# First forms of head 0 and 1 traced ahead of z's, plain output weights loaded as the quads' are, gates loaded behind the last value product: one core, a bidirectional encoder block

## The chip, the cores and the metric

The kernel runs on one core of one Trainium2 chip. The metric is the device time of a launch in microseconds (us). TensorE is called PE, VectorE DVE, ScalarE ACT, GpSimd POOL and SyncE SP; PEld are PE's weight loads.

## The reference

One layer of an encoder on 512 tokens of width 1024, in float32:

```python
h = rmsnorm(x, g_mix);  proj = h @ w_in          # xc, gb, gc, q, k, v, g_sw, gate_a, gate_r
y_a = (gb * dwconv3(gc * xc)) @ w_a_out
ret = retention_fwd(q, k, v) + retention_bwd(q, k, v)       # 4 heads: 256 wide q, k; 512 wide v
ret = (ret - mean) * rsqrt(var + EPS) * g_ret               # per head
y_r = (ret * silu(g_sw)) @ w_r_out                          # 2048 x 1024
x = x + (sigmoid(gate_a) * y_a + sigmoid(gate_r) * y_r) @ w_o
x = x + (silu(h2 @ w_ff_gate) * (h2 @ w_ff_up)) @ w_ff_down # h2 = rmsnorm(x, g_ffn)
return rmsnorm(x, g_final)
```

The change concerns the way to y_r: the value products of the heads, and their output product with w_r_out.

## The kernel before

Every float32 operand is split in two rounded halves, hi and lo (`split`: ACT casts the hi, L217, DVE subtracts for the lo, L218; with a column of scales L220 and L221). A product is three matmuls: hi hi, hi lo, lo hi. Large products run as Strassen's forms, each a sum or difference of blocks that is split in its turn. A matmul of 128x128 by 128x512 is the common one.

**Weights.** `plan` (L64) lists all weight units in the order of use. A quad's unit ("q") comes from the packed array `wquad`: `load_raws` issues its loads on SP's queue ahead of use, up to LEAD (4) entries and more past the one that is being split, into a pool of ten raw tiles (512 KB each). A plain block ("c") comes from `wpack`: `prefetch_block` issues its two loads (L262) at the moment at which it is its turn to be split, two units (AHEAD) before use. Split units (whi, wlo) have five buffers each.

**Queues.** SP's queue carries the loads, and the 16 transfers that turn a head's result into columns (`transpose`, L241, "big<-turned"). POOL's queue carries the stores of z (L668), the accumulating loads of weight sums (L294 to L296), the loads of z's forms (L1054) and the gates A. The framework gives SP's transfers eight semaphores in turn, and a transfer waits until the one before it on its semaphore has landed; it also orders the instructions of each engine, near to the order in which they are traced, and `tc.issue_after` holds an instruction behind another. What is traced first on ACT and DVE is mostly done first, and each engine runs its list in order.

**The stage of the change**, by PE's products in order, with the matmuls of each: scores of head 3 (`do_scores`), `mix_b(3)` (L1094, the last of the convolution's projections, whose results go through `z_forms`), a11 (L1097, 24), a12 (L1100, 24), the value product of head 3 (`do_pv`, L1105, 48), the plain product of head 2 with the right half of its weights (`token_major`, L1110, 48), s1, s2, s3, s4 (24 each), head 2 with the left half (L1131, 48), a22 (24), head 3 with the right half (L1144, 48) and with the left half (L1148, 48); then the products of z (y_a). a11, a12, s1 to s4 and a22 are Strassen's forms of heads 0 and 1 with w_r_out's first 1,024 rows; heads 2 and 3 use its other rows plainly.

- `first_forms` (L1010) makes a11 and a12: two casts on ACT, two subtractions on DVE (128x1024 each). `sum_forms` (L1017) makes s1 and s2, `last_forms` (L1030) s3, s4 and a22.
- `do_pv` normalises each of its four banks: statistics (L967 to L969), the power on POOL (L970), L976 on DVE, which reads the bank for the last time, and L978 on ACT. A bank is free for the next product after L976. `do_t` turns the result on DVE (L238) and on SP (L241), `split_t` splits it with the group norm's gain (L220, L221).
- `leave` (L1117) copies s2's and later s3's banks on ACT (L1119) and subtracts on DVE (L1121).
- `sgr` are the swish gates of the branch R, 8 transfers of 256 KB on SP (`load_turned`, L934, "big<-gr"), traced behind the first `leave`.

Of the kernel before, what the change touches and what calls it, by code (L numbers as in the profile page):

```python
# [17 lines left out]
P = 128  # L18
# [4 lines left out]
HEADS = 4  # L23
QK = 256
VD = 512
# [23 lines left out]
LEAD = 4  # L49
# [2 lines left out]

WIDTH = {"w": 512, "x": 256, "a": 512, "o": 512, "f": 256, "g": 512, "r": 512, "d": 512}
FORMS = ("b11", "t1", "t2", "b21", "t3", "t4", "b22")

EARLY_FORMS = ("b11", "b21", "t1", "t2", "t3", "t4", "b22")
# [5 lines left out]
def plan():  # L64

    out = []

    def a(name, col):
        out.append(("c", name, 0, 8, col, 256))

    def b(name, row, nk, col, nc):
        out.append(("c", name, row, nk, col, nc))

    def quad(c0, c1):
        for name in FORMS:  # L80
            for u in (0, 2):
                out.append(("q", ("w", c0, c1), name, u, 2))

    for h in range(EARLY):
        for r in (0, 512):
            b("w_in", r, 4, (C_Q + h * QK, C_K + h * QK), 512)
    for h in range(HEADS):
        quad(C_V + h * VD, C_G + h * VD)
        if h >= EARLY:
            a("w_in", C_Q + h * QK)  # L90
            a("w_in", C_K + h * QK)
    for c in (0, 512):
        quad(C_GA + c, C_GR + c)
    for c0, c1 in ((C_XC, C_GC), (C_XC + 256, C_GC + 256), (C_GB, C_GB + 256)):
        for name in FORMS:
            out.append(("q", ("x", c0, c1), name, 0, 4))
    for s in (2, 3):
        for c in (C_XC, C_GC, C_GB):
            a("w_in", c + s * 256)
    def r(*names):  # L100
        for name in names:
            for u in (0, 2):
                out.append(("q", ("r",), name, u, 2))

    r("b11", "b21")
    b("w_r_out", 2 * VD, 4, 512, 512)
    r("t1", "t2", "t3", "b22")
    b("w_r_out", 2 * VD, 4, 0, 512)
    r("t4")
    for c in (512, 0):  # L110
        b("w_r_out", 3 * VD, 4, c, 512)
    for kind, name in [("a", x) for x in FORMS[:6]] + [("o", "b11"), ("a", "b22")] + [
            ("o", x) for x in ("t1", "t2", "b21", "b22", "t3", "t4")]:
        for u in (0, 2):
            out.append(("q", (kind,), name, u, 2))
    def f(q, *names):
        for n in names:
            if q == LONE:
                out.append(("q", ("f", q), n, 0, 4))
            else:  # L120
                for u in (0, 2):
                    out.append(("q", ("g", q), n, u, 2))

    def d(q0, n):
        names = FORMS if q0 + n == NQ else EARLY_FORMS
        units = [(name, u) for name in names for u in range(0, n, 2)]
        if q0 + n == NQ:

            i = units.index(("b21", 2))
            units[i:i + 3] = units[i + 1:i + 3] + units[i:i + 1]  # L130
        for name, u in units:
            out.append(("q", ("d", q0), name, u, min(2, n - u)))

    f(0, "b11", "b21")
    f(1, "b11")
    f(0, "t2", "t1", "t3", "t4", "b22")
    f(1, "t1", "t2", "b21", "t3", "t4", "b22")
    f(2, *FORMS)
    d(*FF_PARTS[0])
    f(3, *FORMS)  # L140
    f(4, *FORMS)
    d(*FF_PARTS[1])
    f(LONE, *FORMS)
    d(*FF_PARTS[2])
    return out
# [39 lines left out]
def block_kernel(ctx: ExitStack, tc: tile.TileContext, xw0, xw, xT, xtok, wpack, wquad, cols, decs, gret_rows, rot, g_ffn, g_final, out):  # L185
    nc = tc.nc
# [14 lines left out]
    def bigtile(dt=F32, n=4):  # L201
        return big.tile([P, n, 512], dt, tag="big", name="big", padded_shape=[P, 4, 512])
# [40 lines left out]
    pos = [0]  # L243
# [148 lines left out]

    def token_major(lhs, pss, start, stop):

        c = Chunk()
        for kk in range(4):
            wh, wl = c.w(kk, 0, 512)
            for nb in range(NB):
                xh, xl = (x[:, nb, kk * P:(kk + 1) * P] for x in lhs)
                for i, (l, r) in enumerate(((xh, wh), (xh, wl), (xl, wh))):  # L400
                    nc.tensor.matmul(pss[nb], l, r, start=start[nb] and kk == 0 and i == 0,  # L401
                                     stop=stop[nb] and kk == 3 and i == 2, skip_group_check=True)
# [58 lines left out]
    def snap(ps):  # L461
        t = t512()
        nc.scalar.copy(t, ps)  # L463
        return t
# [189 lines left out]
    sgd = [kept(f"sg{h}") for h in range(HEADS)]  # L654
    gad = [kept(f"ga{j}") for j in range(2)]
    grd = [kept(f"gr{j}") for j in range(2)]
# [16 lines left out]
    for h in range(EARLY):  # L673
        pss = [bank() for _ in range(4)]
        for kk in range(8):
            if kk % 4 == 0:
                c = Chunk()
# [193 lines left out]
    def mix_b(s, c, mid=None):  # L871
        def ev_b(m, ps):
            nc.vector.tensor_tensor(out=c[:, m], in0=ps, in1=c[:, m], op=ALU.mult)
            if mid and not m:
                mid()
        feature_major(xg, ev_b)
        z_forms(s, c)
# [31 lines left out]
    def load(src, dt=F32):  # L909
        t = bigtile(dt)  # L910
        nc.sync.dma_start(t if dt == F32 else t.bitcast(F32), src)
        return t
# [18 lines left out]
    def load_turned(queue, t, d):  # L931

        for j in range(NB):
            queue.dma_start(t[32 * j:32 * j + 32], d[:, j, :].rearrange("(m r) e -> r m e", m=4))  # L934

    def do_scores(qk, tab):
        p = (bigtile(F32R), bigtile(F32R))
        for mb in range(NB):
            ps = bank()
            for d in range(2):  # L940
                sl = slice(mb * P, (mb + 1) * P)
                mm3(ps, (qk[0][:, 2 + d, sl], qk[1][:, 2 + d, sl]), (qk[0][:, d, :], qk[1][:, d, :]),
                    d == 0, d == 1)
            t = t512()
            o = (3 - mb) * P
            nc.vector.scalar_tensor_tensor(out=t, in0=ps, scalar=QK ** -0.5, in1=tab[:, o:o + 512],
                                           op0=ALU.mult, op1=ALU.mult)
            split(t, p[0][:, mb, :], p[1][:, mb, :])
        return p
# [30 lines left out]
    def do_t(h, t):  # L980
        yr = (bigtile(F32R), bigtile(F32R))
        transpose(lambda b: yr[1].bitcast(F32)[:, b, :], t, True)
        return yr
# [58 lines left out]
    def split_t(h, yr):  # L1042
        with tc.issue_after(hi_of[0].ins), tc.issue_after(low_of[0].ins):
            for eb in range(4):
                hi, lo = (x[:, :, P * eb:P * eb + P] for x in yr)
                split(lo.bitcast(F32), hi, lo, gret[:, 4 * h + eb:4 * h + eb + 1])
# [15 lines left out]
    v, sg, g = load_v(0)  # L1062
    p = do_scores(*qk)
# [3 lines left out]
    c = mix_c(2, us)  # L1067

    qk = load_qk(1)
    v, sg1, g = load_v(1)  # L1070
    do_pv(p, vv, sg)
    p = do_scores(*qk)
# [7 lines left out]
    v, sg2, _ = load_v(2)  # L1080
    do_pv(p, vv, sg1)
    p = do_scores(*qk)
# [3 lines left out]
    c = mix_c(3, us)  # L1086

    do_pv(p, vv, sg2)
    v = load(vd[3], F32R)
    p = do_scores(*qk)  # L1090
    yr2 = do_t(2, sg2)
    sg3 = load(sgd[3])
    vv = split_v(v)
    mix_b(3, c, first_forms)  # L1094

    a, b = ([bank(), bank()] for _ in range(2))
    prod_tm(4, rf["a11"], a, True)  # L1097
    p1 = [snap(x) for x in a]
    split_t(2, yr2)
    prod_tm(4, rf["a12"], b, True, True)  # L1100
    ysum.append(bigtile())
# [1 line left out]
        nc.vector.tensor_tensor(out=ysum[0][:, tt, :], in0=b[tt], in1=p1[tt], op=ALU.add)  # L1103
    sum_forms()
    do_pv(p, vv, sg3)  # L1105
    yr3 = do_t(3, sg3)

    new, old = [True] * NB, [False] * NB
    c, e = ([bank(), bank()] for _ in range(2))
    token_major(yr2, e + c, new, old)  # L1110
    last_forms()
    d = [bank(), bank()]
# [8 lines left out]
            nc.vector.tensor_tensor(out=ysum[1][:, o + tt, :], in0=d[tt], in1=u, op=ALU.subtract)  # L1121
        return copies[-1]
    leave(0)
    sgr = [bigtile(), bigtile()]
    for x, src in zip(sgr[::-1], grd[::-1]):
        load_turned(nc.sync, x, src)
    prod_tm(4, rf["s3"], a, False)
    last = leave(2)
    prod_tm(4, rf["s4"], e, False)
# [1 line left out]
    b = [bank(), bank()]  # L1131
# [121 lines left out]
    a, d, b = po["a"], [bank(), bank()], [bank(), bank()]  # L1253
# [254 lines left out]
    n = FF_PARTS[-1][1]  # L1508
# [111 lines left out]
def pack_quads(w_in, w_a, w_r, w_o, gate, up, down):  # L1620

    out = np.zeros((len(QUARTERS), P, QH), np.float32)
    for i, (_, (kind, *q), name, u, n) in enumerate(QUARTERS):
        r, c = int(name[1]) - 1, int(name[2]) - 1
        if kind in "wx":
            w = w_in.reshape(2, 4, P, -1)[r, u:u + n // WIDTH[kind], :, q[c]:q[c] + WIDTH[kind]]
        elif kind == "a":

            w = w_a.reshape(4, 2, P, 2, 512)[u:u + n // 512, r, :, c]
        elif kind == "r":  # L1630
            w = w_r[0:2 * VD].reshape(2, 4, P, 2, 512)[r, u:u + n // 512, :, c]
        elif kind == "o":
            w = w_o.reshape(2, 4, P, 2, 512)[r, u:u + n // 512, :, c]
        elif kind == "f":
            w = (gate, up)[c].reshape(2, 4, P, NQ, 256)[r, :, :, q[0]]
        elif kind == "g":
            w = (gate, up)[c].reshape(2, 4, P, -1)[r, u:u + n // 512, :, q[0] * 512:q[0] * 512 + 512]
        else:
            w = down.reshape(NQ, 2, P, 2, 512)[q[0] + u:q[0] + u + n // 512, r, :, c]
        out[i, :, :n] = w.transpose(1, 0, 2).reshape(P, n)  # L1640
    return out
# [46 lines left out]
```

## Time and profile before

| what | value |
|---|---|
| time, median of 3 runs | 1032.43 us (1031.98 to 1032.61) |
| the profiled execution's own time | 1030.13 us |
| its span, first to last instruction | 1028.3 us |
| mean granted clock of PE | 0.987 |
| instructions | 13417 |
| bytes moved | 222.70 MB, mean 217 GB/s |
| matmul busy | 1001.4 us, x4722 |

The page cuts the span into 40 slices of 25.7 us; slice 20 of them (from 0 to 39) begins at 514 and slice 23 at 591. A row of the timeline gives the start, the duration, the engine, the line, the operation, output<-input by the program's names, how many instructions it joins (x4), and in brackets the idle time before the first of them and what ended it. Starts of neighbouring rows lie closer than durations, since an instruction starts before the end of the one before. The row of a transfer on SPq or POOLq shows when it was issued; when it landed is told by the issues' view (KB of one, median us to landing) or by what waited for it.

### The profile page before, as it was taken

Reading aid. Unit: us, or ns where it says so; the run is one execution under the profiler, and the core shown is the slowest. Engines: PE = TensorE matmul, PEld = TensorE weight load, DVE = VectorE, ACT = ScalarE, POOL = GpSimd, SP = SyncE. Lnnn points to the kernel's source line nnn. Section 1 sums busy time; section 2 is a strip of 40 time slices with the busy share of each in tenths; the row PEclk is TensorE's granted clock in tenths of the full one; section 3 lists DMA queues with packets and bytes.
Section 4 is the critical chain, followed back from the end, with each engine's and each line's share of the span. In section 5 each row is a group of like instructions: output and inputs, shape, how many; then the busy total and the mean of one; then the engine's idle time right before and its main releaser. Section 6 shows DMA issues by size and latency. Waiting matters only on the chain.

```text
span 1028.3 us, 13417 instructions
## 1 busy us (share of the span) xinstructions
PE 1001.4 (97%) x4722; PEld 836.4 (81%) x4722; DVE 876.5 (85%) x1141; ACT 554.3 (54%) x745; POOL 161.0 (16%) x256
## 2 busy tenths in 40 slices
PE   9999999999999999999699989999999999999996
PEld 7888888888889998888578868888888888888885
DVE  7877998979798988967887349999989996999897
ACT  7547656554665445333545215668655555574655
POOL 0030231222112003131302100011001001003202
PEclk9999999999999999999889989999999999999998
DMA  9525587694867657989748987557776459496953
GB/s 352 196 77 196 172 295 220 206 312 144 274 198 234 246 201 248 402 273 243 223 139 214 328 297 224 166 184 210 200 207 155 171 188 258 116 256 113 267 153 103
DMA packets 65795, 222.70 MB, mean 217 GB/s; under 512 B 10240, under 2 KB 10368, under 8 KB 61632
## 3 DMA queue, kind: packets, MB, share of 16 engines
q1 hardware_dynamic: 46816, 149.46, 42.9%
q0 software_dynamic: 18624, 72.10, 26.7%
q8 instruction: 37, 0.61, 0.2%
q10 hardware_dynamic: 288, 0.29, 0.1%
q14 instruction: 30, 0.25, 0.1%
HBM read 173.83 MB, written 57.41 MB: 225 GB/s over the span
## 4 chain that ended last, share of the span: by engine, by line
PE 82%; DMA 8%; DVE 6%; SPq 1%; issue 1%; ACT 1%; POOL 0%; POOLq 0%; ACTq 0%; DVEq 0%
PE bank L456 56%; PE bank L412 8%; PE bank L376 5%; PE bank L377 5%; PE bank L378 5%; DMA big<-turned 2%; DMA big<-gr 2%; DMA raw<-wpack 2%; DMA big<-ql 2%; SPq L241 1%; DVE wlo L218 1%; DVE raw L323 1%; DVE turned L238 0%; DVE big L1142 0%; DVE big L218 0%
## 5 line engine op out<-in xcount | busy, mean ns | idle before, releaser
L218 DVE TENSOR_TENSOR wlo<-raw,whi 128x1024 fp32r<-128x1024 f32 (+2 forms) x306 | 357.8, 1190 | 98.7 <-ACT whi L217 95.6
L217 ACT CAST whi<-raw 128x1024 fp32r<-128x1024 f32 (+2 forms) x305 | 307.8, 1028 | 235.8 <-PE bank L456 82.1
L456 PE MATMUL bank<-whi,xform 128*128 128x512 f32 x1056 | 330.5, 390 | 0.0
L456 PE MATMUL bank<-whi,big 128*128 128x512 f32 x708 | 224.5, 393 | 10.8 <-ACT big L217 9.7
L456 PEld LDWEIGHTS bank<-whi,xform 128*128 128x128 f32 x1056 | 198.0, 188 | 42.2 <-DVE xform L218 1.0
L456 PE MATMUL bank<-wlo,xform 128*128 128x512 f32 x528 | 205.7, 390 | 0.0
L456 PEld LDWEIGHTS bank<-whi,big 128*128 128x128 f32 x708 | 133.8, 189 | 39.9 <-ACT big L217 10.2
L456 PE MATMUL bank<-wlo,big 128*128 128x512 f32 x354 | 138.9, 392 | 0.1
L323 DVE TENSOR_TENSOR raw<-raw 128x1024 f32<-128x1024 f32 x116 | 136.8, 1198 | 0.7
L456 PEld LDWEIGHTS bank<-wlo,xform 128*128 128x128 f32 x528 | 99.1, 188 | 21.1 <-DVE wlo L218 0.7
L463 ACT COPY t<-bank 128x512 f32<-128x512 f32 x97 | 56.6, 586 | 73.9 <-PE bank L456 59.5
L376 PE MATMUL bank<-big,whi 128*128 128x512 f32 x220 | 85.7, 390 | 0.0
L378 PE MATMUL bank<-big,wlo 128*128 128x512 f32 x220 | 85.6, 389 | 0.0
L377 PE MATMUL bank<-big,whi 128*128 128x512 f32 x220 | 85.6, 389 | 0.0
L456 PEld LDWEIGHTS bank<-wlo,big 128*128 128x128 f32 x354 | 67.2, 190 | 14.5 <-DVE wlo L218 0.6
L412 PE MATMUL bank<-xform,whi 128*128 128x256 f32 x304 | 55.3, 283 | 0.2 <-ACT t L463 0.2
L337 POOL DMA_DIRECT2D raw<-wquad x20 | 17.7, 886 | 210.5 <-ACT t L463 66.4
L378 PEld LDWEIGHTS bank<-big,wlo 128*128 128x128 f32 x220 | 41.3, 188 | 8.6
L376 PEld LDWEIGHTS bank<-big,whi 128*128 128x128 f32 x220 | 41.3, 188 | 8.6
L377 PEld LDWEIGHTS bank<-big,whi 128*128 128x128 f32 x220 | 41.3, 188 | 8.6
L412 PEld LDWEIGHTS bank<-xform,whi 128*128 128x128 f32 x304 | 47.5, 192 | 0.7 <-ACT t L463 0.6
L401 PE MATMUL bank<-whi,big 128*128 128x512 f32 x128 | 41.8, 404 | 4.5 <-ACT whi L217 4.5
(218 smaller groups left out, 1299.1 us busy)
## 6 DMA issues: line engine op xcount, KB each, us to landing
raw<-wquad SPq DMA_DIRECT2D x148, 512.0 KB, 5.3
raw<-wpack SPq DMA_DIRECT2D x34, 512.0 KB, 5.8
raw<-wquad POOLq DMA_DIRECT2D x20, 512.0 KB, 6.7
big<-turned SPq DMA_DIRECT2D x112, 64.0 KB, 4.9
t_g<-wquad POOLq DMA_DIRECT2D x12, 512.0 KB, 8.3
z<-t POOLq DMA_DIRECT2D x24, 256.0 KB, 4.6
t_o<-wquad POOLq DMA_DIRECT2D x12, 512.0 KB, 8.1
zform<-z POOLq DMA_DIRECT2D x6, 1024.0 KB, 13.7
```

The costliest lines, as they stand in the source:

```text
L217: first = (round or nc.scalar.copy)(hi, src)
L218: low_of[0] = nc.vector.tensor_tensor(out=lo, in0=src, in1=hi.bitcast(F32), op=ALU.subtract)
L241: nc.sync.dma_start(out(b)[32 * q:32 * q + 32], ts[q // n][32 * b:32 * b + 32, q % n * 512:(q % n + 1) * 512])
L323: nc.vector.tensor_tensor(out=t, in0=t, in1=raws[quad, more, u][:, 0:n], op=ALU.add)
L337: nc.gpsimd.dma_start(out=t[:, 0:n], in_=src[:, 0:n], accum_op=ALU.add)
L376: nc.tensor.matmul(ps, lh, rh, start=first, stop=False)
L377: nc.tensor.matmul(ps, lh, rl, start=False, stop=False)
L378: nc.tensor.matmul(ps, ll, rh, start=False, stop=last)
L401: nc.tensor.matmul(pss[nb], l, r, start=start[nb] and kk == 0 and i == 0, stop=stop[nb] and kk == 3 and i == 2, skip_group_check=True)
L412: nc.tensor.matmul(o, l[:, c], r[:, k], start=start and s == 0 and k == 0 and i == 0, stop=stop and k == 3 and i == 2, skip_group_check=True)
L456: nc.tensor.matmul(pss[tt], l, r[:, c], start=start and k == 0 and i == 0, stop=stop and k == n - 1 and i == 2, skip_group_check=True)
L463: nc.scalar.copy(t, ps)
```

## The change

Three edits. `first_forms` is called right behind the scores of head 3, no more from within `mix_b(3)`; the load of head 3's gates (sg3) is traced later, behind the copies of a11. The plain blocks of w_r_out become units of a new kind "p" of the quads' array, so that `load_raws` issues their loads ahead. And the gates R (`sgr`) are loaded right behind head 3's value product, ahead of its turning, and `load_raws` is called there once more.

```diff
--- before.py
+++ after.py
@@ -52,7 +52,7 @@
 
 
 
-WIDTH = {"w": 512, "x": 256, "a": 512, "o": 512, "f": 256, "g": 512, "r": 512, "d": 512}
+WIDTH = {"w": 512, "x": 256, "a": 512, "o": 512, "f": 256, "g": 512, "r": 512, "p": 512, "d": 512}
 FORMS = ("b11", "t1", "t2", "b21", "t3", "t4", "b22")
 
 EARLY_FORMS = ("b11", "b21", "t1", "t2", "t3", "t4", "b22")
@@ -103,12 +103,11 @@
                 out.append(("q", ("r",), name, u, 2))
 
     r("b11", "b21")
-    b("w_r_out", 2 * VD, 4, 512, 512)
+    out.extend(("q", ("p", 2, 1), "b11", u, 2) for u in (0, 2))
     r("t1", "t2", "t3", "b22")
-    b("w_r_out", 2 * VD, 4, 0, 512)
+    out.extend(("q", ("p", 2, 0), "b11", u, 2) for u in (0, 2))
     r("t4")
-    for c in (512, 0):
-        b("w_r_out", 3 * VD, 4, c, 512)
+    out.extend(("q", ("p", 3, c), "b11", u, 2) for c in (1, 0) for u in (0, 2))
     for kind, name in [("a", x) for x in FORMS[:6]] + [("o", "b11"), ("a", "b22")] + [
             ("o", x) for x in ("t1", "t2", "b21", "b22", "t3", "t4")]:
         for u in (0, 2):
@@ -392,9 +391,10 @@
 
     def token_major(lhs, pss, start, stop):
 
-        c = Chunk()
         for kk in range(4):
-            wh, wl = c.w(kk, 0, 512)
+            if kk % 2 == 0:
+                _, (w,) = take()
+            wh, wl = (x[:, kk % 2 * 512:kk % 2 * 512 + 512] for x in w)
             for nb in range(NB):
                 xh, xl = (x[:, nb, kk * P:(kk + 1) * P] for x in lhs)
                 for i, (l, r) in enumerate(((xh, wh), (xh, wl), (xl, wh))):
@@ -1088,14 +1088,15 @@
     do_pv(p, vv, sg2)
     v = load(vd[3], F32R)
     p = do_scores(*qk)
+    first_forms()
     yr2 = do_t(2, sg2)
-    sg3 = load(sgd[3])
     vv = split_v(v)
-    mix_b(3, c, first_forms)
+    mix_b(3, c)
 
     a, b = ([bank(), bank()] for _ in range(2))
     prod_tm(4, rf["a11"], a, True)
     p1 = [snap(x) for x in a]
+    sg3 = load(sgd[3])
     split_t(2, yr2)
     prod_tm(4, rf["a12"], b, True, True)
     ysum.append(bigtile())
@@ -1103,6 +1104,10 @@
         nc.vector.tensor_tensor(out=ysum[0][:, tt, :], in0=b[tt], in1=p1[tt], op=ALU.add)
     sum_forms()
     do_pv(p, vv, sg3)
+    sgr = [bigtile(), bigtile()]
+    for x, src in zip(sgr[::-1], grd[::-1]):
+        load_turned(nc.sync, x, src)
+    load_raws(pos[0] + LEAD + 2)
     yr3 = do_t(3, sg3)
 
     new, old = [True] * NB, [False] * NB
@@ -1121,9 +1126,6 @@
             nc.vector.tensor_tensor(out=ysum[1][:, o + tt, :], in0=d[tt], in1=u, op=ALU.subtract)
         return copies[-1]
     leave(0)
-    sgr = [bigtile(), bigtile()]
-    for x, src in zip(sgr[::-1], grd[::-1]):
-        load_turned(nc.sync, x, src)
     prod_tm(4, rf["s3"], a, False)
     last = leave(2)
     prod_tm(4, rf["s4"], e, False)
@@ -1627,6 +1629,8 @@
         elif kind == "a":
 
             w = w_a.reshape(4, 2, P, 2, 512)[u:u + n // 512, r, :, c]
+        elif kind == "p":
+            w = w_r.reshape(HEADS, 4, P, 2, 512)[q[0], u:u + n // 512, :, q[1]]
         elif kind == "r":
             w = w_r[0:2 * VD].reshape(2, 4, P, 2, 512)[r, u:u + n // 512, :, c]
         elif kind == "o":
```

How this moves the instructions shows on ACT first, from the scores of head 3 on. Before (big_4453 is v, big_3920 holds heads 0 and 1, so big_4572 are the first forms; t512_46xx are z's):

```order
L217 CAST whi_4660<-raw_4293 128x1024
L217 CAST whi_4694<-raw_4690 128x1024
L217 CAST t512_4606<-big_4289 128x256
L217 CAST t512_4618<-t512_4604 128x512
L217 CAST t512_4624<-t512_4605 128x512
L217 CAST t512_4630<-big_4289 128x256
L217 CAST big_4531<-big_4453 128x1024 x2
L217 CAST big_4572<-big_3920 128x1024 x2
L220 ACTIVATE big_4501<-big_4502,cols_sb_97 128x4x128 x4
```

And in the change (big_4501 are the first forms, big_4535 is v's):

```order
L216 CAST big_4501<-big_3920 128x1024 x2
L216 CAST whi_4660<-raw_4293 128x1024
L216 CAST big_4535<-big_4453 128x1024 x2
L216 CAST t512_4606<-big_4289 128x256
L216 CAST whi_4692<-raw_4540 128x1024
L216 CAST t512_4606<-big_4289 128x256
L216 CAST whi_4710<-raw_4546 128x1024
L216 CAST t512_4618<-t512_4604 128x512
```

The casts of the forms stand ahead of those of the weight and of v, and all of them ahead of z's. The second place is DVE, up to the first L976 of head 3 (before, on bank_4749). Before:

```order
L1026 TENSOR_TENSOR big_3920<-big_3920,t512_4741 128x512
L218 TENSOR_TENSOR big_4730<-t512_4740,big_4729 128x512
L218 TENSOR_TENSOR big_4730<-t512_4741,big_4729 128x512
L967 BN_STATS bnst_4762<-bank_4749 128x6
L218 TENSOR_TENSOR wlo_4876<-raw_3949,whi_4875 128x1024
L968 BN_AGGR bnmv_4763<-bnst_4762 128x2
L1037 TENSOR_TENSOR big_3920<-big_3920,big_3921 128x1024
L969 TENSOR_SCALAR bnmv_4763<-bnmv_4763 128x1
L976 SCALAR_TENSOR_TENSOR big_4529<-bank_4749,bnmv_4763,big_4529 128x512
```

In the change:

```order
L1026 TENSOR_TENSOR big_3920<-big_3920,t512_4741 128x512
L217 TENSOR_TENSOR big_4730<-t512_4741,big_4729 128x512
L967 BN_STATS bnst_4762<-bank_4749 128x6
L967 BN_STATS bnst_4783<-bank_4770 128x6
L968 BN_AGGR bnmv_4763<-bnst_4762 128x2
L967 BN_STATS bnst_4804<-bank_4791 128x6
L969 TENSOR_SCALAR bnmv_4763<-bnmv_4763 128x1
L976 SCALAR_TENSOR_TENSOR big_4680<-bank_4749,bnmv_4763,big_4680 128x512
```

Two more statistics stand ahead of L976, and L1037 (of `last_forms`) has gone behind the value product's rows; the two subtractions of the first forms stand far ahead of this piece, among head 2's transposes. On ACT the three casts of `last_forms`, which came right behind head 3's L978 before, now stand between the first and the second copy of `leave(0)`. The third place is SP's queue around the turning of head 3. Before (gr are the gates R, 4838 head 3's turned tile):

```order
L911 DMA big_4529<-sg3_238 128x2048
L262 DMA raw_5065<-wpack 128x1024
L308 DMA raw_5112<-wquad 128x1024
L241 DMA big_4838<-turned_4839 32x512 x2
L241 DMA big_4838<-turned_4840 32x512 x2
...
L308 DMA raw_5178<-wquad 128x1024
L262 DMA raw_5180<-wpack 128x1024
L262 DMA raw_5181<-wpack 128x1024
L934 DMA big_5017<-gr1_242 32x4x512 x4
L934 DMA big_5016<-gr0_241 32x4x512 x4
L262 DMA raw_5218<-wpack 128x1024
```

In the change (raw_5068 to raw_5140 are the plain weights of head 3, 4848 its turned tile):

```order
L911 DMA big_4680<-sg3_238 128x2048
L307 DMA raw_5005<-wquad 128x1024
L307 DMA raw_5068<-wquad 128x1024
L307 DMA raw_5086<-wquad 128x1024
L934 DMA big_4838<-gr1_242 32x4x512 x4
L934 DMA big_4837<-gr0_241 32x4x512 x4
L240 DMA big_4848<-turned_4849 32x512 x2
L240 DMA big_4848<-turned_4850 32x512 x2
...
L307 DMA raw_5110<-wquad 128x1024
L307 DMA raw_5140<-wquad 128x1024
```

The gates and the first two plain loads of head 3 went ahead of its turning, the last two right behind it. The counts of matmuls and of bytes are those of before.

## Prediction

> **What bounds the kernel now.** I read the page first, then the waits of PE, then the timeline around the two places that these name.
>
> ```profile
> PE 1001.4 (97%) x4722; PEld 836.4 (81%) x4722; DVE 876.5 (85%) x1141; ACT 554.3 (54%) x745; POOL 161.0 (16%) x256
> ...
> PE   9999999999999999999699989999999999999996
> ...
> PEclk9999999999999999999889989999999999999998
> ...
> PE 82%; DMA 8%; DVE 6%; SPq 1%; issue 1%; ACT 1%; POOL 0%; POOLq 0%; ACTq 0%; DVEq 0%
> ```
>
> The reader is to see that PE holds the end: busy 97% of 1028.3 us and 82% of the chain that ended last. One slice of its row inside the program stands at 6 and a later one at 8, and the clock's row drops to 8 with them. The waits of PE between 380 and 640 us, and the windows there (columns: us; PE, PEld, DVE, ACT and POOL busy; granted clock; DMA share; GB/s), say what these are:
>
> ```profile
> PE bank L456 <- ACT big L217: 9.7, 1, 9.7
> PE bank L401 <- ACT whi L217: 4.5, 1, 4.5
> PE bank L456 <- DVE big L218: 1.1, 1, 1.1
> ...
> 510.00:520.00 10.00, 5.78 (x13) 4.10 (x14) 6.10 (x7) 5.26 (x7) 3.33 (x6) 0.50 0.88 278
> 520.00:530.00 10.00, 10.00 (x45) 8.28 (x44) 9.92 (x15) 7.44 (x12) 0.00 (x0) 0.99 0.57 225
> 530.00:540.00 10.00, 10.00 (x45) 8.26 (x45) 10.00 (x21) 2.50 (x4) 1.64 (x3) 1.00 0.01 2
> ...
> 560.00:570.00 10.00, 10.00 (x46) 8.28 (x45) 6.97 (x8) 5.77 (x8) 0.53 (x1) 1.00 1.02 365
> ...
> 600.00:610.00 10.00, 5.93 (x15) 4.37 (x16) 4.08 (x4) 3.98 (x4) 0.00 (x0) 0.66 1.03 303
> ```
>
> Two stalls, then, and each drags a stretch at a lower clock behind it. PE's own timeline gives their price:
>
> ```profile
> 502.80 0.39 PE L377 MATMUL bank<-big,whi 128*128 128x512 f32 x1
> 503.03 0.39 PE L378 MATMUL bank<-big,wlo 128*128 128x512 f32 x1
> 513.15 0.79 PE L456 MATMUL bank<-whi,big 128*128 128x512 f32 x1 [9.73 <-ACT big L217]
> ...
> 517.31 0.63 PE L456 MATMUL bank<-whi,big 128*128 128x512 f32 x1
> 517.74 0.63 PE L456 MATMUL bank<-wlo,big 128*128 128x512 f32 x1
> ...
> 528.22 0.39 PE L376 MATMUL bank<-big 128*128 128x512 f32 x1
> ...
> 539.10 0.39 PE L401 MATMUL bank<-whi,big 128*128 128x512 f32 x1
> ...
> 603.60 0.80 PE L401 MATMUL bank<-whi,big 128*128 128x512 f32 x1 [4.50 <-ACT whi L217]
> ...
> 617.58 0.39 PE L456 MATMUL bank<-whi,zform 128*128 128x512 f32 x1
> ```
>
> A matmul of 512 columns starts 0.227 us after the one before it at full clock (539.10 is 48 of them after 528.22) and 0.43 at half clock (517.31 to 517.74). mix_b(3) ends at 503.26. The 48 matmuls of a11 (L1097) and a12 (L1100) need 10.9 us and end with the value product's start at 528.22, so **stall 1** costs 528.22 - 503.26 - 10.9 = 14.1 us: 9.73 and 1.07 of waiting, the rest half clock. **Stall 2** lies in the last plain product (L1148): PE waits from 599.1, and z's products start at 617.58, so it costs 617.58 - 599.1 - 10.9 = 7.6, of which some 5 are waiting and 2.6 half clock. At stake are 21.7 us.
>
> **What the change removes.** Stall 1 is an order on ACT and DVE:
>
> ```profile
> 498.31 1.22 ACT L217 CAST big<-t 128x512 fp32r<-128x512 f32 x2 [1.01 <-DVE t L946]
> ...
> 510.16 3.88 ACT L217 CAST big<-big 128x1024 fp32r<-128x1024 f32 x4
> ...
> 500.32 2.39 DVE L238 STREAM_TRANSPOSE turned<-big 128x256 f32<-128x256 f32 x7
> ...
> 512.33 4.62 DVE L218 TENSOR_TENSOR big<-big 128x1024 fp32r<-128x1024 f32 x4
> ```
>
> The x4 are two rows for v and two for the first forms, behind the casts of z. In the change's order the two form casts come right behind the scores' last cast, so they end at 499.5 + 2 x 0.97 = 501.5, and their subtractions (4.62/4 = 1.15 each) go in ahead of the last six transposes, from 500.8 to 503.1. PE reaches a11 at 503.3 and finds both: minus 14.1. The margin on the last subtraction is 0.2 us, but only a12 reads it.
>
> Stall 2 is an order on SP:
>
> ```profile
> 561.73 15.42 SPq L934 DMA_DIRECT2D big<-gr x8
> ...
> 582.44 4.13 SPq L262 DMA_DIRECT2D raw<-wpack x2
> ...
> 602.50 1.04 ACT L217 CAST whi<-raw 128x1024 fp32r<-128x1024 f32 x1 [23.54 <-DMA raw<-wpack]
> ```
>
> The last plain weights are issued at 582.44, behind eight gate loads, and the first lands 20 us later. In the change they are the two rows right behind the turning of head 3, which ends some 10 us sooner than before (below): issued by 568, landed by 588 even at 20 us, cast in 1.04, and wanted by PE 10.9 us after head 3's first product, which comes at 588.1 - 14.1 + 7 = 581, so at 592. That is minus 7.6. The packing moves the same 512 KB a load into the same matmuls and costs nothing by itself.
>
> **What the change adds.** First, a **new wait on DVE**. With PE 14.1 us early, the plain product of head 2 wants its third bank at 539.10 + 6 x 0.227 - 14.1 = 526.4. That bank is freed by the first L976 of head 3's value product. Rows of DVE and ACT around it:
>
> ```profile
> 519.54 2.74 DVE L221 SCALAR_TENSOR_TENSOR big<-big,cols_sb 128x512 fp32r<-128x512 f32 x4 [2.59 <-ACT big L220]
> ...
> 522.32 1.23 DVE L218 TENSOR_TENSOR wlo<-raw,whi 128x1024 fp32r<-128x1024 f32 x1
> 523.46 0.68 DVE L1026 TENSOR_TENSOR t<-big 128x512 f32<-128x512 f32 x1
> ...
> 534.94 0.74 DVE L976 SCALAR_TENSOR_TENSOR big<-bank,bnmv,big 128x512 f32<-128x512 f32 x1
> ...
> 518.79 2.56 ACT L220 ACTIVATE big<-big,cols_sb 128x512 fp32r<-128x512 f32 x4 [4.74 <-DMA big<-turned]
> ...
> 542.66 2.94 ACT L217 CAST big<-big 128x1024 fp32r<-128x1024 f32 x3
> ...
> 559.70 0.59 ACT L1119 COPY t<-bank 128x512 f32<-128x512 f32 x1 [0.26 <-PE bank L456]
> ```
>
> Before, L976 ended at 535.7, 4.8 us ahead of PE's need at 540.5. In the change DVE's transposes end 2 x 1.15 later, at 505.0, and from there up to the end of that L976 its order holds 7 rows of 1,024 columns (1.14 from start to start, 522.32 to 523.46), 16 of 512 and 3 statistics (0.60 each by the L1026 rows, 0.08 under the 0.68 of one), 7 of 256 (0.34, by the transposes), the four of L221 (2.7), two scalars (0.15) and the L976: 8.0 + 11.4 + 2.4 + 2.7 + 0.15 + 0.74 = 25.4 us. If none of the waits of before is left in it, L976 ends at 530.4 and PE waits 4.0 us. If head 2's turned tiles land as long after the transposes as before (ACT L220 at 518.79, so 521.1), L221 comes some 1.7 later: 5.7. I take 4.6, nearer to the sum of rows. Behind the waiting matmul stand the product's other banks, s1, s2 and s3; PE takes nothing past it.
>
> Second, the **clock**. Both waits of over 4 us in this stage (9.73, 4.50) had half clock behind them. 4.6 is next to 4.50, so I count a drop. Its price lies between nothing (no drop) and 2.6 as after stall 2; a stretch of 3.4 us at half clock costs 3.4 x (1 - 0.227/0.43) = 1.6, which I take.
>
> The Trainium skill, "TensorE: Matmul & The Clock Gate", under "What's actually happening", has a free-running window of about 3.4 us and a clock that halves after one idle window. By that rule a wait of 4.6 us holds a whole window only for some positions, so the drop is not certain and the sum would be 1.6 us lower without it; the rows of this trace (two of two) speak for the drop.
>
> Third, **last_forms** is late. Its three casts (2.94 us at 542.66, 15 us ahead of use) now stand behind the first copy of leave(0), which waits for a bank of s2. That copy begins at 559.70 where s2 ends at 561.06; 0.5 for it and 0.97 for s3's cast reach 0.1 us past that, and the next cast, 0.97 more, is that of s4. So between 0.1 and 2.0 us; I take 1.0. After a wait this short I count no drop.
>
> Fourth, **the SP queue**. Eight gate loads (2 MB) and three weight loads (1.5 MB) now go out from 518 on, ahead of head 3's 16 turning loads:
>
> ```profile
> 502.45 14.83 SPq L241 DMA_DIRECT2D big<-turned  x16
> 517.38 0.53 SPq L911 DMA_DIRECT2D big<-sg  x1
> ...
> 543.33 13.63 SPq L241 DMA_DIRECT2D big<-turned  x16
> ...
> big<-sg SPq DMA_DIRECT2D x1, 1024.0 KB, 5.3
> ...
> big<-gr SPq DMA_DIRECT2D x8, 256.0 KB, 20.1
> ```
>
> In 520:540 the DMA share was 0.57 and 0.01: there is room. At the rate of sg (1 MB landed in 5.3 us) 3.5 MB need 18.6 us after 518, so they are in at 537, when DVE has head 3's transposes done (530.4 + 6). Turning then takes 13.63 as before and ends at 551, not 557, with 30 us of cover before PE wants head 3 at 581. I cost it at nothing; the other end is the third rival.
>
> **Sum.** -14.1 - 7.6 + 4.6 + 1.6 + 1.0 = -14.5 us. The profiled run took 1030.13 (span 1028.3), so 1015.6; the median of the runs is 1032.43, 2.3 above it, so **1017.9**.
>
> **The rivals.**
> 1. *No new wait of weight.* If a11 starts 1 to 2 us late, or DVE runs its 25.4 us of rows a little shorter, PE's wait falls to 3 us and no clock drops: -21.7 + 3 + 1 = -17.7, so 1014.7; with nothing added, 1010.7. For it: 530.4 and 526.4 are near to each other. Against it: DVE was busy 10.00 of 10 us in 530:540.
> 2. *A longer wait on DVE.* The turned tiles land late, the clock falls for as long as after stall 2, s3 and s4 wait 2: -21.7 + 5.7 + 2.6 + 2 = -11.4, so 1021.0; 1024 with another 3 us at the fourth bank. For it: SP took 14.83 us over head 2's 16 loads.
> 3. *SP's order becomes the bound* (the other side). A transfer takes one of SP's eight semaphores and waits until the one before it there has landed, so the turning loads go out behind two rounds of gate and weight loads. With a latency L for these, head 3 is turned at about 518 + 2L + 9 + 10 and split 3.5 later; PE wants it at 581. It decides from L = 20 us, and each us above costs 2. From L = 27.4 the gain is gone; at 30 the time is 1017.9 + 20 = 1037.9. For it: 20.1 is these loads' own row. Against it: that was measured at a DMA share of 1.02 (560:570), and the new place has 0.57 and 0.01.
>
> The Trainium skill, "DMA: Bandwidth & Descriptors", under "Queues, rings and completion order", has each DMA engine take turns between queue rows. By that the gate loads shared the engines with POOL's loads before and do not now, which is against this rival; no run here shows it yet.
>
> 4. *Only part of it works.* The forms' casts wait for a tile that mix_b(3) still reads, and stall 1 stays: 1032.43 - 7.6 = 1024.8; or the weights are late again and stall 2 stays: 1017.9 + 7.6 = 1025.5. Both: 1032.4, the same. Against it: both moves stand in the order of the engines.
>
> **How the numbers follow.** Forecast (1016 to 1020.5) 0.52; rival 1 (1010.7 to 1016) 0.17; rival 2 (1020.5 to 1024.5) 0.14; rival 3 0.09, of which 0.05 slower than before and 0.01 the same; rival 4 0.08, of which 0.02 the same. About 0.2%, 2.1 us, is what a measurement of this kernel can tell from no change. Faster 0.92, same 0.03, slower 0.05. The range 1011 to 1024 leaves out rival 4, most of rival 3 and the tails of the first two, some 0.18.
>
> **What would show it.** At 503.3 PE goes straight from mix_b into a11, and slice 20 of its row is a 9; else stall 1 was no matter of order. Between 525 and 533 PE has one wait of 4 to 6 us in the plain product of head 2, released by DVE's L976, with a clock under 1.00 behind it: if the wait is missing or the clock whole, rival 1; if over 6, rival 2. At s3 and s4 some 1 us of waiting on ACT's casts. In the last plain products PE waits for no cast. If it waits at head 3's first product for ACT's scaled split, SP's order decides, and the gate loads' time to landing is over 20 us. The prediction is wrong as a whole if DVE cannot bring its rows forward, or if the last plain weights go out after 575.

## The result, and the profile after

The changed kernel takes 1017.59 us (median of 4 runs, 1015.74 to 1019.44) against 1032.52 for the kernel before (4 runs, 1031.98 to 1033.78): a ratio of 0.9854, 95% interval 0.9833 to 0.9874. Run a second time it took 1016.80 against 1033.03, ratio 0.9839 (0.9821 to 0.9856). The forecast was 1017.9.

The profiled execution of the change is its slowest run, 1019.44 us (span 1017.7), and that of before took 1030.13, less than any other run of that kernel, so the two traces stand 10.7 us apart where the medians stand 14.9. A second profile of the change is of a run of 1016.67 us; both are used below.

The page of the change, the same four rows as before:

```profile
PE 999.4 (98%) x4722; PEld 835.1 (82%) x4722; DVE 877.1 (86%) x1141; ACT 555.2 (55%) x745; POOL 161.0 (16%) x256
...
PE   9999999999999999999979999999999999999996
...
PEclk9999999999999999999999999999999999999999
...
PE 89%; DVE 6%; DMA 2%; issue 1%; ACT 1%; SPq 0%; POOL 0%; POOLq 0%; DVEq 0%; ACTq 0%
```

The 6 has gone (it stood in slice 19 counted from 0, 488 to 514 us; the prediction called that one 20) and so has the later 8. One 7 has come, a slice further on, 509 to 534 us. DMA fell from 8% to 2% of the chain: gates and weights no longer end it. The waits of PE between 380 and 640 us, and two windows:

```profile
PE bank L401 <- DVE big L976: 5.6, 1, 5.6
PE bank L401 <- DVE big L1104: 1.2, 1, 1.2
PE bank L456 <- ACT big L216: 0.5, 2, 0.3
...
520.00:530.00 10.00, 7.99 (x34) 5.94 (x33) 8.06 (x13) 4.11 (x7) 0.00 (x0) 1.00 0.99 345
530.00:540.00 10.00, 5.22 (x14) 4.18 (x15) 10.00 (x28) 3.51 (x5) 3.19 (x6) 0.66 1.08 239
```

All five waits of before (9.7, 4.5, 1.1, 0.5, 0.5) are gone; in their place stand the two that the forecast named, L976 and the late forms of s3 and s4 (`ACT big L216`), and a short one on L1104. PE's timeline:

```profile
503.92 0.39 PE L377 MATMUL bank<-big,wlo 128*128 128x512 f32 x1
504.15 0.39 PE L456 MATMUL bank<-whi,big 128*128 128x512 f32 x1
...
515.06 0.39 PE L375 MATMUL bank<-big 128*128 128x512 f32 x1
...
527.99 0.50 PE L401 MATMUL bank<-whi,big 128*128 128x512 f32 x1 [1.20 <-DVE big L1104]
...
534.78 0.80 PE L401 MATMUL bank<-whi,big 128*128 128x512 f32 x1 [5.59 <-DVE big L976]
...
539.61 0.39 PE L401 MATMUL bank<-wlo,big 128*128 128x512 f32 x1
...
607.12 0.39 PE L456 MATMUL bank<-whi,zform 128*128 128x512 f32 x1
```

mix_b(3) runs into a11 with 0.23 us between their starts. From a11's start to z's first product lie 408 matmuls of 512 columns, 92.5 us at 0.2267 each. Before they took 617.58 - 503.26 = 114.3, which is 21.8 over; in the change 607.12 - 504.15 = 103.0, 10.5 over; in the second profile 604.11 - 502.96 = 101.15, 8.7 over. Of the 10.5, 7.3 are the waits above; of the 8.7, 4.60 + 0.5 are. The rest, 3.2 and 3.6, is not all half clock. By the same sum the kernel e7_both (below), with two waits of 0.5 us together and the full clock throughout, took 1.0 us over, and e6_sumlate, with one of 2.56, took 2.9 over: each wait costs some 0.3 us beside its row. With four waits here and three in the second profile that leaves 2.0 and 2.7 us for half clock. So stall 1 and stall 2 went whole, and 8.7 to 10.5 us of the 21.8 came back, nearly all at one place.

That place on DVE and ACT, and SP's queue beside it:

```profile
493.74 2.74 DVE L814 SCALAR_TENSOR_TENSOR big<-u,cols_sb,big 128x512 f32<-128x512 f32 x4 [6.60 <-ACT big L812]
...
505.50 2.07 DVE L237 STREAM_TRANSPOSE turned<-big 128x256 f32<-128x256 f32 x6
...
524.59 2.74 DVE L220 SCALAR_TENSOR_TENSOR big<-big,cols_sb 128x512 fp32r<-128x512 f32 x4 [1.94 <-ACT big L219]
...
533.99 0.73 DVE L976 SCALAR_TENSOR_TENSOR big<-bank,bnmv,big 128x512 f32<-128x512 f32 x1
...
523.84 2.57 ACT L219 ACTIVATE big<-big,cols_sb 128x512 fp32r<-128x512 f32 x4 [5.36 <-DMA big<-turned]
...
507.31 12.05 SPq L240 DMA_DIRECT2D big<-turned  x16
...
523.34 8.71 SPq L934 DMA_DIRECT2D big<-gr  x8
540.05 14.80 SPq L240 DMA_DIRECT2D big<-turned  x16
```

From the end of the transposes (507.57) to the end of L976 (534.72) DVE takes 27.15 us, 1.94 of it waiting for head 2's turned tiles: 25.2 us of rows, where the forecast had counted 25.4. Head 3's turning starts at 540, not 543, behind all the gates; these land 10.9 us after issue, not 20.1.

### The profile page after: what moved, and what is told of

It is laid out like the page before. It is cut to its first block, busy times and chain, and to the rows that moved or that the text cites. A ratio compares the mean times of both kernels' runs of the same rounds, so it can differ in the third digit from the quotient of the medians.

```text
span 1017.7 us, 13414 instructions
## 1 busy us (share of the span) xinstructions
PE 999.4 (98%) x4722; PEld 835.1 (82%) x4722; DVE 877.1 (86%) x1141; ACT 555.2 (55%) x745; POOL 161.0 (16%) x256
## 4 chain that ended last, share of the span: by engine, by line
PE 89%; DVE 6%; DMA 2%; issue 1%; ACT 1%; SPq 0%; POOL 0%; POOLq 0%; DVEq 0%; ACTq 0%
PE bank L456 55%; PE bank L412 8%; PE bank L376 7%; PE bank L375 7%; PE bank L377 7%; PE bank L401 4%; DVE wlo L217 2%; DMA big<-turned 1%; DVE raw L322 1%; DVE big L217 0%; SPq L240 0%; PE bank L512 0%; DMA raw<-wquad 0%; PE bank L1233 0%; PE bank L1179 0%
## 5 line engine op out<-in xcount | busy, mean ns | idle before, releaser
L216 ACT CAST whi<-raw 128x1024 fp32r<-128x1024 f32 (+2 forms) x305 | 308.2, 1029 | 226.1 <-PE bank L456 81.3
```

What stands on the lines that cost most here:

```text
L216: first = (round or nc.scalar.copy)(hi, src)
```

## The experiments

Each time is a median beside runs of the kernel before on the same chip, and each ratio is to that kernel.

### One edit at a time

**e1_forms**, before with the first edit alone:

```diff
     p = do_scores(*qk)
+    first_forms()
     yr2 = do_t(2, sg2)
-    sg3 = load(sgd[3])
     vv = split_v(v)
-    mix_b(3, c, first_forms)
+    mix_b(3, c)
...
     p1 = [snap(x) for x in a]
+    sg3 = load(sgd[3])
```

> The kernel before with the first edit alone: first_forms behind the scores of head 3, sg3 loaded behind a11; plain weights and gates as before. If the two stalls are independent, stall 1 (14.1 us) goes, a wait of 4 to 7 us on DVE's L976 and a stretch at half clock take its place (7 to 9 us in all, as in the trace of the change), and stall 2 (7.6) stays: 1032.5 - 14.1 + 8 = 1026, with PE waiting 4 to 5 us for ACT's cast of a plain weight in the last product. If stall 2 is a lack of time that PE's early start makes worse, it grows by as much as PE is early, and the time is 1030 to 1033.

Measured: 1026.70 against 1032.20, ratio 0.9935 (0.9916 to 0.9954). Its two longest waits of PE in the stage (2.2 us for the lo halves of weights come on top):

```profile
PE bank L401 <- DVE big L976: 5.6, 1, 5.6
PE bank L401 <- ACT whi L217: 3.5, 1, 3.5
```

The wait on DVE comes with this edit alone, and the late weight stays. **e2_noforms** is the change with this edit taken back (the diff above in reverse).

> The change without its first edit: first_forms from within mix_b(3) again, weights and gates as in the change. Stall 1 stays at about 14 us, no wait on L976, stall 2 gone: 1032.5 - 7.6 = 1025. If the gain of the change came from the forms alone, it is 1032.

Measured: 1024.37, ratio 0.9915 (0.9899 to 0.9931), so 7.8 us faster than before, with stall 1 as it was and nothing else:

```profile
PE bank L456 <- ACT big L216: 9.9, 1, 9.9
PE bank L456 <- DVE big L217: 1.4, 1, 1.4
```

The parts add up nearly: 5.5 and 7.8 give 13.3, the whole gave 14.9 and 16.2, with intervals of some 2 us on each side. As far as these times can tell, the two stalls are separate.

### Gates or weights

**e3_nogates** is the change with the gates R loaded behind `leave(0)` again; **e4_noweights** the change with plain blocks again (`b("w_r_out", ...)` in the plan, `c = Chunk()` in token_major).

```diff
-    sgr = [bigtile(), bigtile()]
-    for x, src in zip(sgr[::-1], grd[::-1]):
-        load_turned(nc.sync, x, src)
     load_raws(pos[0] + LEAD + 2)
...
     leave(0)
+    sgr = [bigtile(), bigtile()]
+    for x, src in zip(sgr[::-1], grd[::-1]):
+        load_turned(nc.sync, x, src)
```

> The change without its third edit: the gates R loaded behind leave(0) again, the extra load_raws call kept. If loading the plain weights ahead is what removes stall 2, the time is that of the change, 1017.6, and the last products wait for nothing. If the gates' place is what counts, the last plain weights wait behind them on SP: PE waits some 5 us there and the time is 1024 to 1026.

```diff
-    out.extend(("q", ("p", 3, c), "b11", u, 2) for c in (1, 0) for u in (0, 2))
+    for c in (512, 0):
+        b("w_r_out", 3 * VD, 4, c, 512)
...
-            if kk % 2 == 0:
-                _, (w,) = take()
-            wh, wl = (x[:, kk % 2 * 512:kk % 2 * 512 + 512] for x in w)
+            wh, wl = c.w(kk, 0, 512)
```

> The change without its second edit: the plain weights are plain blocks again, loaded when it is their turn; the gates behind the last value product. If the gates' place is what counts, 1017.6 and no wait in the last products. If loading ahead counts, the last weights are issued at some 580 us as before and PE waits for a cast: 1022 to 1026.

Measured: e3_nogates 1022.60, ratio 0.9902 (0.9887 to 0.9917), which is neither of its two expected times; e4_noweights 1017.03, ratio 0.9848 (0.9831 to 0.9864), which is the change's time. So the gates' move removes all of stall 2, and beside it the packing does nothing that can be measured. Without that move it does something: e3_nogates, with the first edit, the packing and the extra call of `load_raws`, is 4.1 us under e1_forms, which has the first edit alone (1022.60 against 1026.70 on the same chip). In e3_nogates the last products wait for no cast, since the plain weights do come early; the stall has moved on to z's products, whose weights now stand behind the gates. DVE, which makes their lo halves, waits for a load up to 599.87 us and then runs without a pause past PE's wait. SP, the issues' view of 550 to 600 us, DVE, PE:

```profile
553.36 14.21 SPq L934 DMA_DIRECT2D big<-gr x8
...
big<-gr SPq DMA_DIRECT2D x8, 256.0 KB, 22.8
...
599.87 1.23 DVE L322 TENSOR_TENSOR raw<-raw 128x1024 f32<-128x1024 f32 x1 [4.52 <-DMA raw<-wquad]
...
618.75 0.50 PE L456 MATMUL bank<-wlo,zform 128*128 128x512 f32 x1 [2.81 <-DVE wlo L217]
...
621.50 0.80 PE L456 MATMUL bank<-whi,zform 128*128 128x512 f32 x1 [1.25 <-ACT t L463]
```

And SP of e4_noweights, whose plain weights go out at 552 to 561 us though it is only then their turn, the last two 23 us sooner than before, because no gate stands in front:

```profile
521.11 9.40 SPq L934 DMA_DIRECT2D big<-gr x8
...
558.96 2.38 SPq L262 DMA_DIRECT2D raw<-wpack x2
```

### What holds L976

Two theories: the amount of DVE's rows ahead of it (the forecast's), or the landing of head 2's turned tiles, for which L220 waits in front of it. **e5_zlate** calls `z_forms(3, c)` behind `do_pv(p, vv, sg3)` instead of in `mix_b(3)`. **e6_sumlate** calls `sum_forms()` there. **e7_both** does both:

```diff
         feature_major(xg, ev_b)
-        z_forms(s, c)
+        if s != 3:
+            z_forms(s, c)
...
-    sum_forms()
     do_pv(p, vv, sg3)
+    sum_forms()
+    z_forms(3, c)
```

> The change with z's forms of mix_b(3) traced behind head 3's value product, so that 7 rows of 256 and 2 of 512 columns (about 3.6 us on DVE) leave the way to the first L976. If PE's wait there is DVE's amount of work, it falls from 3.9 to 5.6 us to between 0 and 2.5 and the half clock behind it goes: 3 to 6 us faster than the change, 1012 to 1015. If it is the landing of head 2's turned tiles (L220 waits for them), DVE only waits longer ahead of L220, the wait stays over 3 us and the time at 1016 to 1018.

> The change with sum_forms traced behind head 3's value product (6 subtractions of L1026 and 4 of L217, 6 us of DVE). Work theory: wait at L976 under 1.5 us, no half clock; but s3 waits some 2.8 us for last_forms, which are late in turn: 1013 to 1016. Landing theory: 1016 to 1019.

> Both of the last two. Work theory: no wait at L976 over 1 us, clock 1.00 from 500 to 610, s3 and s4 wait 1 us: 4.6 + 1.6 us and a little more than the change gave back, 1010 to 1013. Landing theory: 1016 to 1018.

Measured, against 1032.96: e5_zlate 1012.02, ratio 0.9789 (0.9755 to 0.9823); e6_sumlate 1014.61 (four runs from 1010.95 to 1017.87), ratio 0.9813 (0.9774 to 0.9853); e7_both 1009.81, ratio 0.9767 (0.9738 to 0.9795). In e7_both PE waits in the whole stage only for s3 and s4:

```profile
PE bank L456 <- ACT big L216: 0.5, 2, 0.3
...
505.28 10.14 SPq L240 DMA_DIRECT2D big<-turned  x16
...
516.99 2.57 ACT L219 ACTIVATE big<-big,cols_sb 128x512 fp32r<-128x512 f32 x4 [4.16 <-DMA big<-turned]
...
524.63 0.74 DVE L977 SCALAR_TENSOR_TENSOR big<-bank,bnmv,big 128x512 f32<-128x512 f32 x1
```

L977 here is the change's L976; it ends at 525.4, ahead of PE. At that place e5_zlate waits 0.2 us and e6_sumlate not at all. The amount of rows holds it, then. But moving z's forms did more than take 3.6 us of rows away: six of its eight stores left POOL's queue at that place, and ACT's scaled split now follows SP's first turning load by 11.7 us (505.28 to 516.99), where it was 16.5 in the change (507.31 to 523.84). e6_sumlate kept the stores, its split followed by 14.3 us, and still nothing waited at L976, so the rows alone suffice there; its s3 waited 2.6 us for last_forms, and its runs spread widely.

**e9_split** moves `sum_forms()` and `split_t(2, yr2)` behind the value product, and leaves z's forms:

```diff
     sg3 = load(sgd[3])
-    split_t(2, yr2)
...
-    sum_forms()
     do_pv(p, vv, sg3)
+    split_t(2, yr2)
+    sum_forms()
```

> The change with sum_forms and the split of head 2's turned tiles both traced behind head 3's value product: L976 of the first banks no longer stands behind L220, so neither 6 us of work nor the landing of the turned tiles holds it. Both theories: no wait at L976; last_forms late, s3 waits 3 to 4 us: 1013 to 1016. If it is faster than the kernel with sum_forms alone moved by 2 us or more, the landing has its part.

Measured: 1015.42, ratio 0.9822 (0.9795 to 0.9850). PE still waited 1.0 us at L976, where none was expected, 2.6 for s3's form and 0.7 behind it. It was not faster than e6_sumlate, so this gives the landing no part; what it lost on last_forms hides whether it has a small one.

**e14_nostores** separates the two without moving a row of DVE:

```diff
             for d, x in zip(zd[j], hl):
-                store(d[:, :, s, :], x.rearrange("p (f t) -> p f t", f=n).bitcast(F32))
+                for to in ((s, 3) if s == 2 else () if s == 3 else (s,)):
+                    store(d[:, :, to, :], x.rearrange("p (f t) -> p f t", f=n).bitcast(F32))
```

> The change, in which the eight stores of z's last quarter leave out their data: they go out with the third quarter's, from its tiles, some 60 us earlier, so that the output is not the reference's. DVE's rows and their order stay as in the change. This takes the stores away from beside head 2's turning loads. If these loads are late because the stores share the engines, ACT's scaled split follows SP's first turning load by 11.7 us, as in the kernels with z's forms traced late, and not by 14.3 to 16.5; DVE then has no wait ahead of L220, and PE's wait at L976 shrinks by what that wait was, 0.6 to 1.9 us, to about 4: 1015 to 1016.5. If the landing is the larger part of PE's wait, and the amount of DVE's rows the smaller, the wait falls under 2 us and the time to 1012.

Measured: 1019.80, ratio 0.9867 (0.9847 to 0.9887), slower than the change. The time was a miss of both theories, but the trace answers the question, and shows a third thing:

```profile
508.61 10.41 SPq L240 DMA_DIRECT2D big<-turned  x16
...
520.53 2.56 ACT L219 ACTIVATE big<-big,cols_sb 128x512 fp32r<-128x512 f32 x4 [1.02 <-DMA big<-turned]
...
495.04 2.74 DVE L814 SCALAR_TENSOR_TENSOR big<-u,cols_sb,big 128x512 f32<-128x512 f32 x4 [8.71 <-ACT big L812]
...
534.04 0.71 PE L401 MATMUL bank<-whi,big 128*128 128x512 f32 x1 [3.41 <-DVE big L977]
```

Without the stores the split follows SP by 11.9 us (508.61 to 520.53), and DVE does not wait for it. So the stores do delay the landing: the split follows by 14.3 to 16.5 us in e6_sumlate and the two profiles of the change, which have all eight there, and by 11.7 to 13.5 in this kernel and the three with z's forms traced late, which have none or two. But the doubled stores of the third quarter, some 60 us earlier, delay head 1's turning loads. In that stretch SP is held up, big<-v goes out at 459 us instead of 452 in e15_change, and big<-ql behind it takes 20.1 us to land instead of 16.5; the turning loads wait for that one. ACT's L812 waits for them and DVE's L814 behind it: DVE starts this stretch at 495.0, and all that follows is late. PE waits 0.92 and 0.66 us at a11, and the clock falls there as well (last section).

**e15_change** is the change again, **e16_best** the same as e7_both, on one chip.

> The change itself once more, beside the best version on the same chip: 1017.6, its runs spread over some 3 us. A second profile shows the wait at L976 as long as DVE's end of head 2's transposes is late: end of the transposes plus 25.4 us and what L220 waits.

> The change with z's forms of mix_b(3) and sum_forms traced behind head 3's value product: 1009.8 as before, with no wait at L976 and the clock at 1.00 from 500 to 610, and its runs closer together than those of the change, since PE has slack against DVE again.

Measured: e15_change 1016.80 (1016.48 to 1017.94), e16_best 1009.16 (five runs, 1008.79 to 1011.23), ratio to the kernel before 0.9768 (0.9750 to 0.9787). e16_best beats both kernels: 23.9 us under before, 7.6 under the change. Its spread was not smaller than that of the change here (2.4 against 1.5), so that part of the expectation does not hold, nor do the 3 us expected for the change. The second profile of the change has L976 end at 531.0 us, which is the end of the transposes (504.8) plus 25.2 us of rows and 1.0 of waiting, as expected:

```profile
490.95 2.74 DVE L814 SCALAR_TENSOR_TENSOR big<-u,cols_sb,big 128x512 f32<-128x512 f32 x4 [4.99 <-ACT big L812]
...
520.88 2.74 DVE L220 SCALAR_TENSOR_TENSOR big<-big,cols_sb 128x512 fp32r<-128x512 f32 x4 [1.03 <-ACT big L219]
...
530.27 0.74 DVE L976 SCALAR_TENSOR_TENSOR big<-bank,bnmv,big 128x512 f32<-128x512 f32 x1
531.07 0.80 PE L401 MATMUL bank<-whi,big 128*128 128x512 f32 x1 [4.60 <-DVE big L976]
```

Three profiles with the same rows on DVE now tell what PE waits for. From the start of L814 to the end of the first L976: 40.98 us in the change, 40.06 in e15_change, 38.94 in e14_nostores. Less the wait ahead of L220 (1.94, 1.03, none) that is 39.04, 39.03 and 38.94: DVE runs 39.0 us of rows from the landing of head 1's turned tiles on, and PE's wait is that sum, plus the wait for head 2's tiles, less PE's own way.

## Why the prediction was right

- **Stall 1 goes (-14.1).** Right: a11 follows mix_b(3) at once in the change; e1_forms has no wait there, and e2_noforms, without the edit, has 9.9 and 1.4.
- **Stall 2 goes (-7.6).** Right in size (e2_noforms, 7.8) and in cause, the order on SP. The prediction had the plain weights' own place behind head 3's turning do it; e4_noweights shows that the gates' move does it alone, and e3_nogates that early plain weights without it hand most of the stall on to z's weights (5.6 us over e4_noweights).
- **The packing costs nothing.** Right: e4_noweights, without it, takes the change's time. It gains something only where the gates stay behind (e3_nogates).
- **The new wait on DVE (+4.6).** Right in place, engine and line, and in DVE's rows (25.2 counted against 25.4). In size 6.8 in the first profile (5.59 and the 1.20 on L1104, which stands behind L220 in DVE's order) and 4.6 in the second. What was taken from before as fixed, the end of the transposes at 505.0, lay at 507.6 and 504.8; the bound of 5.7 had the late turned tiles, not this.
- **The clock (+1.6).** Right that it drops; mis-sized: 2.0 and 2.7, and the 0.3 us at the edges of each wait, 1.2 and 0.9 together, had no term at all. The prediction priced one stretch of 3.4 us at half clock. In both profiles it lasted 6.8 us, during the first 2.6 and 1.1 of which PE still waited. The trace of before had no stretch of 3.4 us in this stage either: its two lasted 13.7 and 6.8. The upper end that was given, 2.6, was the better guess. Every profiled wait of 3.41 us or more in this stage had a drop with it; the last section shows why.
- **last_forms (+1.0).** 0.5 of waiting in two waits, whose edges are counted above.
- **SP's queue (0).** Right; rival 3 fell: the gates landed in 10.9 and 10.5 us, far under the 20 from which it would have decided. (At its own 2 us for each one above 20, the gain would be gone from 27.3 on, not 27.4.)

The sum was -14.5 and the medians gave -14.9 and -16.2, though the terms that came back were 8.7 to 10.5, not 7.2, and the profiled runs moved by 10.7 and 13.5. So it is partly luck that the forecast lies within 0.4 us of the first median. The profile of before was 2.4 us under the median of that kernel's runs, and the prediction carried that gap over unchanged, while the second profile of the change lies at its median: the gap covered the terms that were too small. No trace shows where the slower runs of before spend those 2 us; that their stall 1 is longer is a guess.

## What to carry to other kernels

When a stall of PE is removed, add up the rows that the next engine has to run from its last own wait up to the next bank that PE needs: here 25 us of DVE rows stood where PE left 21 (505.0 to 526.4), and that difference, with the clock behind it, was most of the price. Tracing work that is needed later behind the normalisation (z's forms, s1 and s2) gave back 7.6 us more. Loads that others wait behind belong into a stretch where the DMA engines have room: there each gate load landed in half the time, and the weights behind them came early without any change of their own. Undo each part of a change alone, and try it alone too: the packing did nothing beside the gates' move and, with its extra call of `load_raws`, 4.1 us without it.

## What the runs showed of the hardware

The granted clock of every trace changes only on a grid of 3.41 us, which lies differently in each run. Half clock lasted one step of it in e4_noweights and e9_split and twice in e14_nostores, two steps in both profiles of the change and behind stall 2 of before, and four behind stall 1. What counts is how long PE worked within a step. Two steps each of e14_nostores, e6_sumlate and e9_split, in the columns of before:

```profile
503.45:506.86 3.41, 1.83 (x8) 1.16 (x8) 3.41 (x6) 3.41 (x4) 1.62 (x2) 1.00 0.61 156
506.86:510.27 3.41, 3.41 (x10) 2.64 (x9) 3.41 (x9) 2.08 (x4) 0.00 (x0) 0.50 0.89 151
...
545.30:548.71 3.41, 2.13 (x10) 1.44 (x8) 1.23 (x1) 2.33 (x4) 0.67 (x2) 1.00 1.05 211
548.71:552.12 3.41, 2.12 (x9) 1.67 (x10) 3.09 (x3) 3.13 (x4) 0.43 (x1) 1.00 1.07 236
...
549.00:552.41 3.41, 0.73 (x2) 0.30 (x2) 2.52 (x3) 3.39 (x5) 1.10 (x2) 1.00 0.89 196
552.41:555.82 3.41, 2.83 (x7) 2.25 (x8) 3.41 (x5) 0.98 (x2) 0.32 (x1) 0.50 1.07 240
```

In e14_nostores two waits of 0.92 and 0.66 us fell into one step, PE worked 1.83 us of it, and the next step had half clock. e6_sumlate and e9_split both had a wait of 2.56 us. In e6_sumlate it lay across two steps, with 2.13 and 2.12 us of work, and the clock stayed; in e9_split it lay in one, with 0.73, and the clock fell. Over all traces, apart from the last 30 us of the programs, a drop came behind every step with 1.83 us of work or less and behind none with 2.12 or more; the clock came back behind a step with 2.83 us or more and not behind one with 2.37 or less. In those last 30 us two steps with 1.55 and 1.80 us had no drop, so busy time alone does not set the limit sharply. A wait of 3.41 us or more leaves at most 1.7 us of work in one of the steps that it touches, which is why each of these had its drop.

The Trainium skill, "TensorE: Matmul & The Clock Gate", under "What's actually happening", has a free-running window of about 3.4 us and a clock that halves after one idle window. The grid and the lengths agree with it; but the window need not be idle throughout, since PE worked 1.83 us in the one of e14_nostores.

A gate load took 20.1 to 22.8 us to land in its old place, beside POOL's loads of z's forms, and 8.3 to 10.9 in the new one, apart from them; head 2's turning reached ACT after 14.3 to 16.5 us beside POOL's eight stores and after 11.7 to 13.5 with two or none. The Trainium skill, "DMA: Bandwidth & Descriptors", under "Queues, rings and completion order", has each DMA engine take turns between queue rows. These times agree with that; no run here shows the turns themselves.
